# A fifth weight tile, gathers on GpSimd, one state buffer, and solve visits that wait for TensorE's instruction count

## The chip, the cores and the metric

The kernel runs on one core of a Trainium2 chip. The metric is the device time of one execution in microseconds; the median of several runs counts. Beside it stands one profiled execution, from which all views of the profile come.

## The reference

One step of a small decoder: an RWKV-7 layer (layer A) and an attention layer (layer B), on a prompt of 16 meta tokens and 256 tokens and on 8 single-token samples (280 columns in all), all in float32. Width of the model 2048, inner width 4096, 64 heads of 64.

```python
rkvz = jnp.einsum('btpd,pde->btpe', xm[:, :, :4], w_rkvz)      # four 2048 x 4096 products
w_log = -jax.nn.softplus(-(w0 + jnp.tanh(xw @ w1) @ w2)) - 0.5
decay = jnp.exp(-jnp.exp(w_log));  a = jax.nn.sigmoid(a0 + (xa @ a1) @ a2)
kk = normalized(k_h * k_k);  k_h = k_h * (1 + (a_h - 1) * k_a);  b_h = kk * a_h
def rwkv7_step(S, inp):                                         # scanned over the tokens, per head
    r, d, k, v, kk, b = inp
    sa = jnp.einsum('bhij,bhj->bhi', S, kk)
    S = S * d[:, :, None, :] - sa[..., None] * b[:, :, None, :] + v[..., None] * k[:, :, None, :]
    return S, jnp.einsum('bhij,bhj->bhi', S, r)
y = (group_norm(y) + bonus) * jax.nn.silu(z);  out_A = y @ w_out
k, v = shared_kv(h)                                             # for layer B
out_B = (banded attention with sinks(q, k, v) * jax.nn.silu(z)) @ w_o
```

Outputs are the normed hidden states, the recurrent states of prompt and samples, the shifts and the key and value caches.

## The kernel before

Activations lie transposed, features on partitions and the 280 columns along the free axis. Every large product is made of three TensorE passes (`mm3`): a weight tile `raw` of 128x512 comes in by DMA (`wunits`, line 200), ScalarE rounds it to `whi` (line 184), VectorE forms the rest `wlo` (line 186), and whi x xhi, whi x xlo, wlo x xhi are added in PSUM (lines 207 to 209). `raw` has 4 buffers, `whi` and `wlo` 5. SyncE's queue issues nearly all DMAs, in order.

Phase A (`phase_a`, `drive`) weaves layer A together. `products` runs 64 products (r, k, v, z in a fixed order, then the first half of the output product, `ps_o`), each in 16 pieces of six matmuls. `drive` turns a loop: at each turn every stream that is due issues its next part, and then one piece of a product follows. A stream says `yield n` (come back n turns later), or `yield n, condition`. TensorE's order is exactly the order of issue. The streams are:

- `main`: for each of eight groups of 8 heads (`o`) the scores of the odd unit, `substitute` (VectorE and POOL invert 16x16 triangles from the masked tile `ND`), `solve`, then `chain` (five steps over the tokens). `solve` makes the inverse larger in four visits to TensorE of short matmuls on 32-row quarters: two of 64 matmuls with 16 columns (lines 1082 and 1088), two of 32 matmuls with 32 columns (1100 and 1109), between them copies on VectorE and ScalarE. It begins `yield 24 if o < 5 else 27`, and `yield 4`, `7`, `5` stand between its visits.
- `preps`: prepares a unit of two pairs of heads: low-rank products `ps_l`, loads of `kT`, `rT`, `kk`, `vT`, and the gather of the samples' columns into `sm` by six ScalarE copies of 128x16 (line 910), which a transpose `ps_sm` (913) reads 8 turns later.
- `even_scores`, `group_norm` (transposes `ps_yt`, 1239, then the store of `yd`), `epilogues`.
- `decodes`: four groups of samples; each loads eight parts `dS` of the old state (1271), makes two products with each (1275), sums them (1276), and ends in a transpose `ps_dy` (1299).
- `late_gates`: once the last chain step and the fourth decode are done, splits the gated outputs of heads 32 to 63 into `ghi` and `glo` (lines 184, 186), which the second half of the output product, `ps_oa` in `out_a`, reads from its first matmul on.

In `scores`, ScalarE copies three 32-row parts of a score bank per half: two into `ND` (lines 997 and 998) and one into `N12` (999), a tile of its own; `solve` reads `N12` at line 1100.

Layer B (`phase_b`, `out_b`) follows with products `ps_kv`, `ps_q`, `ps_z`, `ps_ob`.

```python
# decode, before
S = rp.tile([128, NI, 64], F32, tag="dS", bufs=2, name=f"dS{g}_{q}")
...
dma(S.rearrange("p i j -> p (i j)"), I['state_wkv'][...])
yield 8 if g < 3 else 5, lambda: self.samples
for w, o in ((kk, sa), (dr, y)):
    tt(T, S, rowb(w), op=MU)
    V.reduce_sum(o[:, iq], T, axis=AX.X)
```

Of the kernel before, what the change touches and what calls it, by code (L numbers as in the profile page):

```python
# [107 lines left out]

class Kernel:
    def __init__(self, nc, tc, I, O):  # L110
        self.nc, self.tc, self.I, self.O = nc, tc, I, O
# [76 lines left out]
    def wunits(self, w, name, nk, col, nc_, per):  # L188
# [3 lines left out]
        for k0 in range(0, nk, per):  # L192
# [5 lines left out]
            else:  # L198
                raw = t("raw", F32, bufs=4)
# [5 lines left out]
    def mm3(self, ps, wh, wl, xh, xl, start, stop):  # L205
        mm = self.nc.tensor.matmul
# [23 lines left out]
    def gemm32(self, w, name, nk, cols, x):  # L230
# [4 lines left out]
        for k0 in range(0, nk, 2):  # L235
            for c, col in enumerate(cols):
# [3 lines left out]
                for k in range(2):  # L240
                    for i in range(2):
                        self.lead = self.nc.tensor.matmul(ps[2 * c + i][:, :N], raw[:, k, 128 * i:128 * i + 128],
                                                          x(k0 + k), start=k0 + k == 0, stop=k0 + k == nk - 1).ins
# [50 lines left out]
    def phase0(self):  # L294
# [23 lines left out]
        def filling(n):  # L318
            for _ in range(n):
                nc.tensor.matmul(junk[:, :N], ones, fill, start=True, stop=True)  # L320

        def summed(*ks):
            for k in ks:
                nc.tensor.matmul(pss[:, :N], ones, sq[:, k], start=k == 0, stop=k == KT - 1)
# [73 lines left out]
        def lora1():  # L398

            self.lt = []  # L400
            for m, wn, pool in ((4, 'a_w1', self.pc), (5, 'a_a1', self.pp)):
                ps = self.bank(pool, f"ps_{wn}")[:LR, :N]
                wv = self.I['lw'][:, m - 4]
                for k0 in range(0, KT, 4):
                    raw = lw0 if m == 4 and k0 == 0 else lw(f"{m}_{k0}")
                    dma(raw, wv[:, k0:k0 + 4])
                    for k in range(4):
                        if k % 2 == 0:
                            t = raw_part(m, (k0 + k) // 2)
                        nc.tensor.matmul(ps, raw[:, k], t[:, k % 2], start=k0 + k == 0, stop=k0 + k == KT - 1)  # L410
# [94 lines left out]
    def squares(self, p0, sqs):  # L505
        nc = self.nc
        pk = self.bank(self.py, f"ps_kk{p0}")
        for j in range(2):
            nc.tensor.matmul(pk[:, :N], self.sel[j], sqs[j], start=j == 0, stop=j == 1)
# [6 lines left out]
    def turn_v(self, p0, j, t, vk):  # L516
        nc = self.nc
        pt = self.bank(self.pe, name=f"ps_vt{p0}_{j}")
        for i, r in enumerate((128, 128, 16)):
            nc.tensor.transpose(pt[:r, i * 128:i * 128 + 128], t[:, j, i * 128:i * 128 + r], self.ident)  # L520
# [38 lines left out]
    def phase_a(self):  # L559
# [7 lines left out]
        self.ND = t([128, 20, 32], "ND")  # L567
# [6 lines left out]
        for a in (self.KB, self.ND, self.N16, self.Noff, self.Y):  # L574
            ms(a, 0.0)
# [229 lines left out]
    def end_k(self, p0, t):  # L805
# [6 lines left out]
        for j in range(2):  # L812
            nc.tensor.matmul(pk[:, :N], self.sel[j], sq[:, j], start=j == 0, stop=j == 1)
# [8 lines left out]
    def end_v(self, p0, t):  # L822
# [3 lines left out]
        for j in range(2):  # L826
            yield 3, self.pp_free
            pt = self.pp_bank(f"ps_vt{p0}_{j}")
            for i, r in enumerate((128, 128, 16)):
                nc.tensor.transpose(pt[:r, i * 128:i * 128 + 128], t[:, j, i * 128:i * 128 + r], self.ident)  # L830
# [5 lines left out]
    def prep(self, u):  # L836
# [72 lines left out]
        for i, x in enumerate((kk, a, kT, rT, vT, Pp[:, :, 5:])):  # L909
            A.copy(sm[:, :, i], x[:, :, L:N])  # L910
        yield 8, self.pp_free
        ps = self.pp_bank(f"ps_sm{u}")
        nc.tensor.transpose(ps[:96, :128], sm.rearrange("p a b c -> p (a b c)"), self.ident)
# [12 lines left out]
        for j in range(2):  # L926
            yield 5 - j if u > 1 else 3, self.pp_free
            ps = self.pp_bank(f"ps_bo{j}_{u}")
            nc.tensor.matmul(ps[:, :L], self.cr[C_BO], rk[j], start=True, stop=True)
# [30 lines left out]
    def scores(self, u):  # L960
# [15 lines left out]
        if u % 2 == 0:  # L976
            self.N12 = rp.tile([128, 16, 32], F32, tag="N12", name=f"N12_{u}")
        N12 = self.N12
# [3 lines left out]
        for c0 in (0, 2):  # L982
# [4 lines left out]
            with self.pe_order():  # L987
                for j in range(2):
                    for c in range(2):
                        for q in (1, 0):  # L990
                            o = 128 * (c0 + c)
                            nc.tensor.matmul(ps[q][:, j, c], KB[H(q), j, c0 + c, 64 * q:64 * q + 128],
                                             E[q][H(q), j, o:o + 128], start=True, stop=True)
            for q in range(2):
                pv, kr, br = ps[q], H(1 - q), H(q)
                r1, r2 = slice(64 * q, 64 * q + 32), slice(64 * q + 32, 64 * q + 64)
                A.copy(inst(self.ND, r1, cs), pv[r1, :, :, 0:32])
                A.copy(inst(self.ND, r2, cs), pv[r2, :, :, 32:64])
                A.copy(inst(N12, r1, cs), pv[r1, :, :, 32:64])
# [6 lines left out]
        with self.pe_order():  # L1006
            for j in range(2):
                for q in (1, 0):
                    nc.tensor.matmul(ps[q][:, j], KB[H(q), j, 4, 64 * q:64 * q + 128], E[q][H(q), j, 512:544],
# [13 lines left out]
        for j in range(2):  # L1023
            yield next(gap)
            ps = [b[:, :320].rearrange("p (c t) -> p c t", c=5) for b in banks(("bk", f"{j}_{u}"))]
            with self.pe_order():
                for c in range(5):
                    for q in (1, 0):
                        nc.tensor.transpose(ps[q][:, c], KB[H(q), j, c, 64 * q:64 * q + 128], self.ident[H(q), H(q)])
# [39 lines left out]
    def solve(self, o):  # L1069
# [16 lines left out]
        for i in range(16):  # L1086
            for q in range(4):
                nc.tensor.matmul(ps[32 * q:32 * q + 16, 256 + 16 * i:272 + 16 * i], ET[Q[q], i], TR[Q[q], :, i],
# [9 lines left out]
        for i in range(16):  # L1098
            for q in range(2):
                nc.tensor.matmul(ps[Q[2 * q + 1], i], self.N12[Q[2 * q], i], TN2[Q[2 * q], i], start=True, stop=True)  # L1100
# [5 lines left out]
        for i in range(16):  # L1106
            for q in range(2):
                r = Q[2 * q + 1]
                nc.tensor.matmul(ps[Q[2 * q], i], ET[r, i], TT[r, i, 32:64], start=True, stop=True)
# [27 lines left out]
    def chain(self, o):  # L1137
# [10 lines left out]
        mm = nc.tensor.matmul  # L1148
# [769 lines left out]
```

## Time and profile before

| | |
|---|---|
| median of 3 runs | 2190.12 us (2186.92 to 2193.9) |
| the profiled execution | 2201.98 us |
| its span | 2200.2 us |
| TensorE busy | 2122.6 us, 96% |
| VectorE busy | 1716.4 us, 78% |
| ScalarE busy | 1272.9 us, 58% |
| POOL busy | 83.4 us, 4% |
| mean granted clock of TensorE | 0.985 |

The views give times in microseconds from the span's start. A row of the time line reads: start, duration, engine, line of the code, operation, tiles written and read, shapes, count, and in brackets the idle time before it with what ended it. A row of the waits reads: total, times, longest. A row of a tile reads: minimum, median and maximum in ns, first and last start. A row of the stretches gives each engine's busy time with its number of instructions, the granted clock, and the share and rate of the DMA engines. "issue" is waiting for nothing that the profile shows. A DMA queue's row (q8) gives packets, MB and share.

### The profile page before, as it was taken

The page shows a single profiled execution, that of the slowest core. Times are in us where ns is not written, and L with a number is a line of the kernel's source. Part 1 is how long each engine was busy: PE and PEld are TensorE (multiplying, and loading weights), DVE is VectorE, ACT ScalarE, POOL GpSimd, SP SyncE. Part 2 cuts the span into 40 slices and gives each one's busy share as a digit, 9 for nine tenths or more (in the row PEclk, how much of TensorE's full clock was granted, in tenths as well). Part 3 has the DMA queues.
Part 4 walks back from the last instruction along what each step waited for, and adds up shares of the span by engine and source line. Part 5 has one row for each costly group of instructions (what it writes and reads, how often), then busy time and mean ns, then how long its engine had stood idle before and what let it go on. Part 6 is the DMA issues. An engine that isn't in the chain of part 4 may idle for free.

```text
span 2200.2 us, 56108 instructions
## 1 busy us (share of the span) xinstructions
PE 2122.6 (96%) x21556; PEld 2015.7 (92%) x21556; DVE 1716.4 (78%) x4115; ACT 1272.9 (58%) x2916; POOL 83.4 (4%) x100
## 2 busy tenths in 40 slices
PE   9999999999999998999999999999999999999997
PEld 7998899999889898888889899998999999999997
DVE  7956767787587776877887786997888888888885
ACT  3456756675666656756666454564565556555443
POOL 0010000000000000100001000110000000000000
PEclk9999999999999999999999999999999999999999
DMA  6997667757656776665645878766554544577774
GB/s 235 320 316 233 191 192 236 210 175 258 198 171 187 235 226 178 203 196 173 207 138 156 276 228 251 241 213 200 157 160 139 168 145 135 167 209 242 231 225 136
DMA packets 277444, 448.51 MB, mean 204 GB/s; under 512 B 53352, under 2 KB 99112, under 8 KB 276784
## 3 DMA queue, kind: packets, MB, share of 16 engines
q1 hardware_dynamic: 276888, 443.89, 65.1%
q8 instruction: 169, 2.77, 0.5%
q10 hardware_dynamic: 288, 1.05, 0.1%
q14 instruction: 99, 0.81, 0.1%
HBM read 382.81 MB, written 66.15 MB: 204 GB/s over the span
## 4 chain that ended last, share of the span: by engine, by line
PE 82%; DMA 6%; DVE 6%; ACT 4%; issue 2%; SPq 0%; DVEq 0%; POOLq 0%; ACTq 0%
PE ps_z L207 6%; PE ps_z L208 5%; PE ps_z L209 5%; PE ps_ob L209 3%; PE ps_ob L208 3%; PE ps_v L207 3%; PE ps_ob L207 3%; PE ps_q L209 3%; PE ps_q L207 3%; PE ps_q L208 3%; PE ps_k L207 3%; PE ps_v L208 3%; PE ps_v L209 3%; PE ps_k L209 2%; PE ps_k L208 2%; PE ps_r L207 2%
## 5 line engine op out<-in xcount | busy, mean ns | idle before, releaser
L207 PE MATMUL ps_z<-mhlm,whi_z 128*128 128x280 f32 x512 | 160.9, 314 | 1.1 <-ACT st L770 1.1
L208 PE MATMUL ps_z<-mhlm,whi_z 128*128 128x280 f32 x512 | 152.2, 297 | 2.1 <-issue 2.1
L207 PE MATMUL ps_q<-bmh,whi_qb 128*128 128x264 f32 x512 | 150.5, 294 | 2.4 <-ACT whi_qb L184 2.4
L209 PE MATMUL ps_z<-mhlm,wlo_z 128*128 128x280 f32 x512 | 152.0, 297 | 0.0
L209 PE MATMUL ps_q<-bmh,wlo_qb 128*128 128x264 f32 x512 | 146.7, 286 | 1.5 <-DVE wlo_qb L186 1.5
L207 PE MATMUL ps_z<-bmh,whi_zb 128*128 128x264 f32 x512 | 147.5, 288 | 0.0
L208 PE MATMUL ps_q<-bml,whi_qb 128*128 128x264 f32 x512 | 146.1, 285 | 0.0
L208 PE MATMUL ps_z<-bml,whi_zb 128*128 128x264 f32 x512 | 145.5, 284 | 0.0
L209 PE MATMUL ps_z<-bmh,wlo_zb 128*128 128x264 f32 x512 | 145.5, 284 | 0.0
L207 PE MATMUL ps_ob<-ghi,whi_ob 128*128 128x264 f32 x512 | 145.3, 285 | 0.0
L209 PE MATMUL ps_ob<-ghi,wlo_ob 128*128 128x264 f32 x512 | 144.9, 285 | 0.0
L208 PE MATMUL ps_ob<-glo,whi_ob 128*128 128x264 f32 x512 | 144.5, 283 | 0.0
L186 DVE TENSOR_TENSOR wlo_r<-raw_r,whi_r 128x512 fp32r<-128x512 f32 x128 | 87.8, 688 | 64.9 <-ACT whi_r L184 63.9
L184 ACT CAST whi_oa<-raw_oa 128x512 fp32r<-128x512 f32 x128 | 78.9, 620 | 101.2 <-DMA raw_oa<-a_w_out 31.7
L184 ACT CAST whi_ob<-raw_ob 128x512 fp32r<-128x512 f32 x128 | 79.2, 621 | 97.1 <-PE ps_ob L208 80.2
L186 DVE TENSOR_TENSOR wlo_v<-raw_v,whi_v 128x512 fp32r<-128x512 f32 x128 | 87.9, 691 | 53.0 <-ACT whi_v L184 48.7
L207 PE MATMUL ps_k<-mhlm,whi_k 128*128 128x280 f32 x384 | 121.9, 317 | 1.9 <-ACT whi_k L184 1.6
L207 PE MATMUL ps_v<-mhlm,whi_v 128*128 128x280 f32 x384 | 121.4, 316 | 1.9 <-ACT st L770 1.9
L186 DVE TENSOR_TENSOR wlo_z<-raw_z,whi_z 128x512 fp32r<-128x512 f32 x128 | 88.6, 695 | 35.7 <-ACT whi_z L184 32.7
L186 DVE TENSOR_TENSOR wlo_oa<-raw_oa,whi_oa 128x512 fp32r<-128x512 f32 x128 | 87.5, 689 | 35.4 <-ACT whi_oa L184 31.7
L186 DVE TENSOR_TENSOR wlo_k<-raw_k,whi_k 128x512 fp32r<-128x512 f32 x112 | 76.0, 687 | 49.5 <-ACT whi_k L184 49.1
L184 ACT CAST whi_zb<-raw_zb 128x512 fp32r<-128x512 f32 x128 | 78.3, 619 | 62.5 <-PE ps_z L208 42.0
(462 smaller groups left out, 7739.5 us busy)
## 6 DMA issues: line engine op xcount, KB each, us to landing
raw_k<-a_w_rkvz SPq DMA_DIRECT2D x128, 256.0 KB
raw_v<-a_w_rkvz SPq DMA_DIRECT2D x128, 256.0 KB
raw_r<-a_w_rkvz SPq DMA_DIRECT2D x128, 256.0 KB
raw_z<-a_w_rkvz SPq DMA_DIRECT2D x128, 256.0 KB
raw_oa<-a_w_out SPq DMA_DIRECT2D x128, 256.0 KB
raw_qb<-b_w_qz SPq DMA_DIRECT2D x128, 256.0 KB
raw_zb<-b_w_qz SPq DMA_DIRECT2D x128, 256.0 KB
raw_ob<-b_w_o SPq DMA_DIRECT2D x128, 256.0 KB
```

What stands on the lines that cost most here:

```text
L184: self.nc.scalar.copy(hi, src)
L186: return self.nc.vector.tensor_tensor(lo, src, hi.bitcast(F32), op=ALU.subtract)
L207: mm(ps, wh, xh, start=start, stop=False)
L208: mm(ps, wh, xl, start=False, stop=False)
L209: return mm(ps, wl, xh, start=False, stop=stop)
```

## The change

Five things change. `raw` has 5 buffers. The six gathers into `sm` go from ScalarE to GpSimd. `ND` and `N12` become the two halves of one tile `F`, so that one copy of 64 columns takes the place of two of 32. `dS` has one buffer; its load comes 3 turns after the products of the part before, and these follow 5 turns later (4 in the fourth group). And a wrapper `TensorE` counts every matmul and transpose that is issued, with an assumed duration, in blocks of 256 instructions; the first two visits of `solve` ask it ahead of each quarter whether the rest of the visit leaves the block at least 5000 ns long, and otherwise come back a turn later.

```diff
+class TensorE:
+    BLOCK = 256
+    def __init__(self, tensor):
+        self.tensor, self.n, self.at = tensor, 0, 0.0
+        self.left = 190.0
+    def count(self, n, ns):
+        self.n += n
+        self.left -= n * 1.004
+        self.at += ns
+        if self.left <= 0:
+            self.left += self.BLOCK
+            self.at = 0.0
+    def matmul(self, out, lhsT, rhs, **k):
+        c = 1
+        for x in rhs.shape[1:]:
+            c *= x
+        exact = rhs.dtype == F32
+        self.count(4 if exact else 2, (17 if c <= 16 else 33 if c <= 32 else 68 if c <= 64 else c) if exact else c * .46)
+        return self.tensor.matmul(out, lhsT, rhs, **k)
+    def transpose(self, out, in_, ident):
+        self.count(2, 45)
+        return self.tensor.transpose(out, in_, ident)
+    def room(self, n):
+        m = min(n, self.left)
+        return self.at + 4.3 * m + 64 * (self.left - m) >= 5000
...
-                raw = t("raw", F32, bufs=4)
+                raw = t("raw", F32, bufs=5)
...
-        self.ND = t([128, 20, 32], "ND")
+        self.F = t([128, 20, 64], "F")
+        self.ND, self.N12 = self.F[:, :, 0:32], self.F[:, 0:16, 32:64]
...
-            A.copy(sm[:, :, i], x[:, :, L:N])
+            G.tensor_copy(sm[:, :, i], x[:, :, L:N])
...
-                A.copy(inst(self.ND, r1, cs), pv[r1, :, :, 0:32])
+                A.copy(inst(self.F, r1, cs), pv[r1, :, :, 0:64])
                 A.copy(inst(self.ND, r2, cs), pv[r2, :, :, 32:64])
-                A.copy(inst(N12, r1, cs), pv[r1, :, :, 32:64])
...
         for i in range(16):
+            while i % 4 == 0 and not self.te.room(256 - 16 * i):
+                yield 1
             for q in Q:
-                nc.tensor.matmul(ps[q, 16 * i:16 * i + 16], Noff[q, i], TN[q, :, i], start=True, stop=True)
+                self.te.matmul(ps[q, 16 * i:16 * i + 16], Noff[q, i], TN[q, :, i], start=True, stop=True)
...                                       # the same loop around the second visit
         for q in range(64 // NI):
-            S = rp.tile([128, NI, 64], F32, tag="dS", bufs=2, name=f"dS{g}_{q}")
+            if q:
+                yield 3
+            S = rp.tile([128, NI, 64], F32, tag="dS", bufs=1, name=f"dS{g}_{q}")
...
-            yield 8 if g < 3 else 5, lambda: self.samples
+            yield 5 if g < 3 else 4, lambda: self.samples
```

Every other `nc.tensor.matmul` and `nc.tensor.transpose` becomes `self.te.matmul` and `self.te.transpose`, with the same operands.

More of the change, by code (lines that the diff above doesn't have):

```diff
@@ L409, in lora1 @@
                             t = raw_part(m, (k0 + k) // 2)
[L410 removed]
+                        self.te.matmul(ps, raw[:, k], t[:, k % 2], start=k0 + k == 0, stop=k0 + k == KT - 1)
                     if k0 < KT - 4:
@@ L1414, in out_a @@
             if k >= KT - 2:
-                nc.tensor.matmul(pst[:, :N], ones, acc if k == KT - 2 else sq, start=k == KT - 2,
+                self.te.matmul(pst[:, :N], ones, acc if k == KT - 2 else sq, start=k == KT - 2,
                                  stop=k == KT - 1)
```

74 lines of the change are left out of this document (37 added, 37 removed).

## The prediction

> **What bounds the kernel now.** I read the page's head first, then TensorE's waits, then the clock by stretch, then the places the change touches.
>
> ```profile
> span 2200.2 us, 56108 instructions
> PE 2122.6 (96%) x21556; PEld 2015.7 (92%) x21556; DVE 1716.4 (78%) x4115; ACT 1272.9 (58%) x2916; POOL 83.4 (4%) x100
> q8 instruction: 169, 2.77, 0.5%
> PE 82%; DMA 6%; DVE 6%; ACT 4%; issue 2%; SPq 0%; DVEq 0%; POOLq 0%; ACTq 0%
> ```
>
> TensorE is busy 96% of the span and carries 82% of the chain: time is won only where it idles or runs slowly. Each recorded matmul has a weight load beside it, so 2 x 21556 instructions came in 169 fetches, 255 each: a block is 256.
>
> ```profile
> PE ps_so L1088 <- issue: 5.5, 4, 1.8
> PE ps_z L208 <- issue: 2.1, 1, 2.1
> PE ps_o L207 <- issue: 2.0, 1, 2.0
> PE ps_so L1109 <- ACT ET L1104: 4.6, 3, 1.9
> PE ps_vt L830 <- ACT ta L861: 2.9, 2, 2.0
> PE ps_so L1088 <- DVE ET L1084: 2.3, 1, 2.3
> PE ps_v L207 <- ACT st L770: 1.9, 1, 1.9
> PE ps_sy L1184 <- ACT X L1183: 1.6, 1, 1.6
> ```
>
> In TensorE's waits (total, times, longest) 9.6 us are "issue": nothing in the profile was awaited. The rest are short waits for ScalarE and VectorE. Nearly all lie in phase A, whose clock the stretches show (PEclk stands behind the engines, before DMA share and GB/s):
>
> ```profile
> 350.00:650.00 300.00, 291.16 (x3490) 271.06 (x3489) 225.48 (x521) 198.58 (x490) 12.89 (x16) 0.97 0.66 208
> 650.00:950.00 300.00, 284.51 (x3560) 265.39 (x3558) 230.03 (x521) 192.60 (x454) 14.18 (x12) 0.98 0.69 207
> 950.00:1240.00 290.00, 270.70 (x3492) 252.81 (x3493) 230.06 (x512) 181.78 (x425) 13.32 (x12) 0.97 0.60 187
> 411.50:414.80 3.30, 3.30 (x16) 3.21 (x15) 3.30 (x6) 2.11 (x5) 0.00 (x0) 0.50 0.76 200
> 804.10:807.40 3.30, 3.30 (x16) 3.30 (x16) 1.83 (x3) 1.11 (x3) 0.00 (x0) 0.50 0.50 143
> 831.40:834.70 3.30, 3.30 (x14) 3.30 (x15) 3.05 (x9) 0.41 (x2) 0.00 (x0) 0.50 1.04 343
> 967.90:974.60 6.70, 6.70 (x92) 6.37 (x88) 2.77 (x5) 3.02 (x7) 0.00 (x0) 0.50 0.61 165
> 1097.60:1100.90 3.30, 3.30 (x16) 3.27 (x15) 1.83 (x3) 1.35 (x4) 0.00 (x0) 0.50 0.63 204
> ```
>
> TensorE idles 8.8, 15.5 and 19.3 us there, and the clock loss adds 9, 6 and 8.7 us. The last five rows show how: stretches of about 3.3 us (one of 6.7) at half clock, half of which is lost, about 1.7 us for a short one. The one at 804.1 begins right behind this stall:
>
> ```profile
> 800.79 0.93 PE L1088 MATMUL ps_so<-TR,ET 32*16 32x16 f32 x91
> 802.87 0.48 PE L1088 MATMUL ps_so<-TR,ET 32*16 32x16 f32 x37 [1.16 <-issue]
> ```
>
> The 128 records (256 instructions, one block) of a solve's visit need only 0.93 + 0.48 us. The stall sits in their middle, and the only thing that comes in such blocks is the code itself.
>
> **The hold (`room`).** It removes the cause of 9.6 us if the count hits the true borders. I take 8, for some drift of the count; bounds 0 and 9.6. The half-clock stretches at 804 and 1098, both behind a second visit's stall, go with it: 2 x 1.7 = 3.4.
>
> Its price is lateness. `main` is paced by its own yields: chain 48 turns of the drive, odd scores 21, solve 40 (43 from the fifth), all else behind them. A turn emits one piece, six product matmuls; 64 products of 16 pieces make 1024. I counted both kernels' turns and instructions by the code's yields and conditions, positions only. For the kernel before, the fourth decode's ps_dy comes at piece 962, the last ps_yt at 988, the last gate at 992: 32 turns of room. For the changed kernel each visit is checked four times. Example, first solve: 42 instructions left, at 13682 ns, so it starts; after 64 instructions it is in a new block, 192 to go, 234 left, and 4.3 x 192 + 64 x 42 = 3514 is under 5000. A piece adds 773 ns and takes 12 instructions, so little changes until 192 are left, then 721 are gained each: five turns. The eight solves give 5+1, 6+2, 2+1, 5+2, 3+2, 0+8, 0+8, 0+8: **53 turns**, all kept to the end, since `main` waits for nobody. The last ps_yt moves to 1041, 17 turns past the last product. The fourth decode starts 53 later too, and its eight loads now need 7 turns each instead of 5: ps_dy at 1030, gates at 1036 to 1046. All gates, which the first ps_oa needs, fall behind the last product. What happens there now (the time line; the row of four casts is the tile ghi's):
>
> ```profile
> 1300.55 0.27 PE L1299 MATMUL ps_dy<-consts,dy 128*64 128x128 f32 x1
> 1305.13 1.13 ACT L184 CAST ghi<-gy 128x1120 fp32r<-128x1120 f32 x1 [0.68 <-DVE gy L1367]
> 1323.49 0.49 PE L1239 MATMUL ps_yt<-consts,Y 128*128 128x128 f32 x3
> L184 ACT CAST ghi<-gy x4: 1122/1124/1129, 1305.1 to 1337.1; 128x1120 fp32r<-128x1120 f32 x4
> 1353.48 0.29 PE L207 MATMUL ps_oa<-ghi,whi_oa 128*128 128x280 f32 x1
> ```
>
> A turn lasts (1353.48 - 1300.55) / 62 = 0.85 us here. The last state step (emitted 16 turns before ps_dy) would come 10 turns, 8.5 us, before the products end, and its arithmetic takes 16 turns (13.7 us) as now: ps_dy stands 5 us past the end. From ps_dy to the end of the first ghi are 1306.26 - 1300.55 = 5.7 us. So TensorE has nothing to do for 11 us. From the last ps_yt to the last ghi are 1338.2 - 1323.5 = 15 us, against about 9 us until its first use in ps_oa; some 2 us of stall follow. Idle TensorE brings at least one half-clock stretch, 1.7. Together 15, and 2 for the loads below: **17 us**, bounds 0 (if everything is early) and 26.
>
> **One state buffer.** A load may now start only when the second product of the step before has read the tile (the time line, then two pieces of the chain of waits, start and length):
>
> ```profile
> 1258.55 0.68 DVE L1275 TENSOR_TENSOR dT<-dS,ve 128x512 f32<-128x512 f32 x1
> 1259.99 0.69 DVE L1275 TENSOR_TENSOR dT<-dS,ddr 128x512 f32<-128x512 f32 x1
> 741.58 5.94 DMA raw_k<-a_w_rkvz
> 747.58 9.82 DMA raw_k<-a_w_rkvz
> ```
>
> Two products last 2.1 us, the load of 256 KB 5 to 10 us (raw tiles of the same size on the chain, thus late ones; I take 5). The sum, 7 to 8 us, is above the seven turns of the fourth decode (6 to 7) and under the eight of the others (9 at their 1.18 us, 1210 us by 1024 turns). Behind the waiting load stand raw loads on SP's queue; behind the waiting product stand the lo splits on VectorE. Besides the 2 us in the tail I take 1; bounds 0 and 8.
>
> **Gathers to POOL.** On ScalarE they cost little by themselves and much by what they wait for (the rows of the tile sm with the idle time ahead of its readers and writers, then the time line):
>
> ```profile
> L910 ACT COPY sm<-vT x16: 198/204/208, 158.3 to 1099.7; 128x16 f32<-128x16 f32 x16
>   DMA rT<-rd: 24.7, 15
>   DMA vT<-vd: 15.2, 8
> 945.46 0.20 ACT L910 COPY sm<-vT 128x16 f32<-128x16 f32 x1 [3.12 <-DMA vT<-vd]
> 949.31 0.69 DVE L186 TENSOR_TENSOR wlo_z<-raw_z,whi_z 128x512 fp32r<-128x512 f32 x1 [4.74 <-ACT whi_z L184]
> 951.21 1.24 PE L1088 MATMUL ps_so<-TR,ET 32*16 32x16 f32 x128 [2.27 <-DVE ET L1084]
> ```
>
> 96 copies of 0.2 us are 19 us, and ScalarE stood 40 us in front of them for two loads. The last three rows are the damage: ScalarE waits 3.12 us for vT, VectorE then 4.74 for ScalarE, and TensorE 2.27. The five listed waits for ScalarE and VectorE are 13.3 us; looking back up to 7 us on ScalarE's time line, such a gather stands ahead of all but one of the three for ET L1104 (1.35, half of what its longest leaves) and the longer one for ta (2.0): 10 us. I take 8, bounds 0 and 13. Half-clock stretches follow such waits at 411, 831 and 968 (two long): 4 x 1.7 = 6.8, of which I take 5. On POOL the copies get in front of the masks on which the solve rests; the nearest row bounds one from above, ScalarE's 0.2 us from below:
>
> ```profile
> L1411 POOL COPY sqacc<-sqa 128x280 f32<-128x280 f32 x1 | 0.4, 427 | 73.5 <-ACT sqa L1408 73.5
> ```
>
> Six are 1.2 to 2.6 us per unit, inside the 8 turns left for them ahead of ps_sm; POOL is 4% busy. Cost 1, bounds -1 and 5.
>
> **Copies.** Two of 256 ns become one twice as wide; at equal width 16x256 took 363:
>
> ```profile
> L998 ACT COPY ND<-ps_sc x64: 256/257/263, 192.1 to 1190.6; 32x128 f32<-32x128 f32 x64
> L1092 ACT COPY TT<-ps_so x16: 362/364/366, 270.4 to 1230.9; 16x256 f32<-16x256 f32 x16
> ```
>
> 64 x 150 ns are 9.6 us off ScalarE, off the path; with 19 us of gathers gone as well, I credit 4 us of the remaining short waits (0 to 10). **The fifth raw tile** starts each load one unit earlier; I credit 3 us (0 to 6) for late raw loads like the 9.82 above.
>
> **The sum.** Gains 8 + 3.4 + 8 + 5 + 4 + 3 = 31; costs 17 + 1 + 1 = 19. The profiled execution took 2201.98 us (span 2200.2) and would take 2190. The median of the runs, 2190.12, lies 11.9 below it; the same 12 us off give **2178**. 0.3% is 6.6 us, about what a measurement can tell.
>
> **Rivals.** *Slower, the tail decides:* the single state buffer makes each of the last seven loads 2 us later (9.8 us for a landing), so ps_dy, and with it every gate, comes 14 us later than I put it, and the waits merely move: costs 33, and of the gains the 5, 4 and 3 that I only credited don't come, 19 left: 2204. It decides once the tail exceeds the gains, 31 us at my values. For it: 53 turns against 32 of room, and nothing in the code brings `main` forward. Against: the decode's VectorE work gets thinner when no products run. *The hold does nothing:* the stalls are not fetches, or the count misses them: without 11.4 us of gain it is 2190, no change. The stall inside one instruction's run speaks against it. The Trainium skill, in "Runtime: NRT & Kernel Launch", section "Instruction fetch mechanics", says that the next 16 KiB block of 256 instructions is fetched while the present one runs and that crossing is mostly hidden; by it the hold is worth nothing. The trace agrees on the size and not on the hiding (1.16 us in mid-visit). *The tail is hidden:* the gates still come early, 17 us less: 2161. *The gathers stall POOL:* the masks wait behind vT, and the solve with them: the 13 us of that item are lost, 2191. The skill's "SBUF — State Buffer", section "Who interferes with whom", has a VectorE operation with two SBUF inputs block against a POOL read; no run here shows it for such copies.
>
> **How the numbers follow.** Forecast 0.45, slower rival 0.27, idle hold 0.12, hidden tail 0.08, POOL 0.08. The forecast's own spread is 11 us either way, so a fifth of it is no change and a twentieth slower. Faster: 0.34 + 0.08 + 0.05 from the edges of the others = 0.47. Slower: 0.27 + 0.02 + 0.04 = 0.33. Same: 0.20. The range reaches from the hidden tail to just past the slower rival, 2161 to 2206; the faster cases' own range is 2161 to 2183.
>
> **What would show it.** The issue rows of ps_so gone; no gather on ScalarE, and its waits for rT and vT on POOL; the half-clock stretches fewer; eight solves drifting late, the last ps_dy and ps_yt behind the last ps_o, and a gap of 11 to 20 us ahead of the first ps_oa. If that gap is missing, my turns are wrong; if phase A's products end no earlier than now, the gains are.

## The result, and the profile after

| | before | after |
|---|---|---|
| median | 2191.13 us (6 runs, 2186.92 to 2194.7) | 2164.4 us (6 runs, 2158.35 to 2172.02) |
| ratio | 1 | 0.988 (95% interval 0.9856 to 0.9905) |
| profiled execution | 2201.98 us | 2161.31 us |

The change makes the kernel 26.7 us faster. The prediction said faster, by 12 us. The two profiled executions lie 40.7 us apart, because that of before was 11 us above its median and that of after 3 below; so terms of a few us are taken from the medians of runs below, not from these two traces.

The head of the page after, and the engines of its chain:

```profile
span 2159.5 us, 56146 instructions
PE 2104.0 (97%) x21556; PEld 2003.4 (93%) x21556; DVE 1714.4 (79%) x4115; ACT 1258.4 (58%) x2756; POOL 137.0 (6%) x196
PE 75%; DMA 5%; DVE 4%; ACT 2%; issue 1%; SPq 0%; DVEq 0%; POOLq 0%; ACTq 0%; POOL 0%
```

160 instructions left ScalarE (96 gathers, 64 copies), and 96 came to POOL. The three stretches of phase A that the prediction showed, in the kernel after:

```profile
350.00:650.00 300.00, 297.57 (x3617) 278.99 (x3616) 233.34 (x543) 199.79 (x455) 32.25 (x44) 1.00 0.69 214
650.00:950.00 300.00, 290.33 (x3755) 272.61 (x3754) 241.07 (x537) 199.37 (x432) 26.26 (x38) 0.99 0.70 219
950.00:1240.00 290.00, 282.36 (x3647) 265.27 (x3647) 237.80 (x517) 179.67 (x390) 19.58 (x30) 0.99 0.64 196
```

TensorE now idles 2.4, 9.7 and 7.6 us (8.8, 15.5 and 19.3 before), and the clock is at 1.00, 0.99 and 0.99 (0.97, 0.98, 0.97). TensorE's waits (total, times, longest), some rows:

```profile
PE ps_oa L130 <- ACT ghi L217: 4.8, 1, 4.8
...
PE ps_so L130 <- DVE TN L1091: 2.6, 2, 2.3
...
PE ps_wu L130 <- ACT X L1234: 2.4, 4, 0.8
...
PE ps_sm L134 <- POOL sm L944: 2.3, 1, 2.3
...
PE ps_z L130 <- issue: 1.4, 1, 1.4
```

The "issue" waits on ps_so are gone (before: 5.5 us), of the others one of 1.4 us is left. A new wait leads the list: the first reader of the late gate's cast `ghi`. (In this kernel every matmul is issued from the wrapper's line 130 and every transpose from line 134, so go by the tiles.) The tile ps_oa, first and last start, before and then after:

```profile
L209 PE MATMUL ps_oa<-ghi,wlo_oa x256: 287/292/299, 1353.7 to 1452.7; 128*128 128x280 f32 x128
```

```profile
L130 PE MATMUL ps_oa<-ghi,wlo_oa x256: 286/292/435, 1303.1 to 1417.6; 128*128 128x280 f32 x128
```

Up to the first ps_oa the profiled execution gains 50.6 us (1353.7 to 1303.1); the ps_oa stage, taken here and below from the first to the last start of this row, loses 15.5 (99.0 becomes 114.5: the tail); layer B gains the remaining 5.6. That sets the questions: what gave 50.6, and was it the hold, which also made the tail?

### The profile page after: what moved, and what is told of

Same layout as the page of the kernel before. It is cut to its first block, busy times and chain, and to the rows that moved or that the text cites. A ratio compares the mean times of both kernels' runs of the same rounds, so it can differ in the third digit from the quotient of the medians.

```text
span 2159.5 us, 56146 instructions
## 1 busy us (share of the span) xinstructions
PE 2104.0 (97%) x21556; PEld 2003.4 (93%) x21556; DVE 1714.4 (79%) x4115; ACT 1258.4 (58%) x2756; POOL 137.0 (6%) x196
## 4 chain that ended last, share of the span: by engine, by line
PE 75%; DMA 5%; DVE 4%; ACT 2%; issue 1%; SPq 0%; DVEq 0%; POOLq 0%; ACTq 0%; POOL 0%
PE ps_z L130 18%; PE ps_ob L130 9%; PE ps_q L130 7%; PE ps_k L130 7%; PE ps_r L130 5%; PE ps_v L130 5%; PE ps_oa L130 4%; PE ps_o L130 3%; PE ps_sy L130 3%; PE ps_wu L130 2%; PE ps_kv L130 2%; PE ps_so L130 2%; PE ps_at L130 1%; PE ps_sc L130 1%; DMA dS<-state_wkv 1%
## 5 line engine op out<-in xcount | busy, mean ns | idle before, releaser
L130 PE MATMUL ps_z<-mhlm,whi_z 128*128 128x280 f32 x1024 | 210.8, 301 | 2.7 <-issue 1.4
L130 PEld LDWEIGHTS ps_z<-mhlm,whi_z 128*128 128x128 f32 x1024 | 162.4, 189 | 8.2 <-issue 1.8
L130 PE MATMUL ps_v<-mhlm,whi_v 128*128 128x280 f32 x768 | 160.4, 303 | 0.0
L130 PE MATMUL ps_k<-mhlm,whi_k 128*128 128x280 f32 x768 | 158.4, 301 | 0.0
L130 PEld LDWEIGHTS ps_v<-mhlm,whi_v 128*128 128x128 f32 x768 | 121.4, 189 | 4.3 <-ACT st L804 0.2
L130 PEld LDWEIGHTS ps_k<-mhlm,whi_k 128*128 128x128 f32 x768 | 121.5, 188 | 4.1
L217 ACT CAST whi_v<-raw_v 128x512 fp32r<-128x512 f32 x128 | 78.7, 618 | 65.3 <-PE ps_v L130 30.4
```

The lines of the kernel that those rows point to most:

```text
L130: return self.tensor.matmul(out, lhsT, rhs, **k)
L217: self.nc.scalar.copy(hi, src)
```

## The experiments

Two theories at the start. A: ScalarE's relief (gathers, copies) is the gain that was sized too small. B: the hold is the large gain. C, that the fifth raw tile is, stood as an outsider. Times below are medians beside the kernel before on the same chip; differences in us between runs of different sets go by their ratios to it (0.001 is 2.2 us).

### The hold

Without it, all else kept:

```diff
-            while i % 4 == 0 and not self.te.room(256 - 16 * i):
-                yield 1
```

> The changed kernel without the two waits of the solve's long visits; fifth raw tile, gathers on POOL, merged copies and the single state buffer stay. The first ps_oa stage falls back from 115 to about 99.5 us (16 us won), since main is no longer late. Theory A (ScalarE's relief is the gain that I sized too small, some 35 us of it): only the six issue stalls and two half-clock stretches return, 10 to 13 us, so the time is about 2160 (2157 to 2165), and the products still end about 1310 us. Theory B (the hold is the large gain: it takes away fetch stalls and, with them, most half-clock stretches, 35 us and more): the products end at 1340 us and the time is about 2185. Prediction as on record: 11.4 us of gain gone and 17 of cost gone, 2159.

Measured: 2155.92 us, ratio 0.9849 (0.9826 to 0.9873), that is faster than the full change. TensorE's waits and the ps_oa stage of this run:

```profile
PE ps_so L130 <- issue: 3.0, 4, 1.3
...
PE ps_r L130 <- issue: 1.8, 1, 1.8
```

```profile
L130 PE MATMUL ps_oa<-ghi,wlo_oa x256: 287/292/299, 1314.6 to 1413.5; 128*128 128x280 f32 x128
```

The products end 11.5 us later than with the hold (1314.6 beside 1303.1), and the stage is 15.6 shorter (98.9 beside 114.5). Theory B falls: in this pair of traces the hold brings 11.5 us, where 11.4 was on record, and its tail costs more. The hold alone, on the kernel before:

> The kernel before with the instruction count and the waits of the long visits alone; four raw tiles, gathers on ScalarE, separate copies, two state buffers. Theory A: the issue stalls and two half-clock stretches go (11 us), the late gates cost 16, so about 2196 (2192 to 2200). Theory B: 35 us go and 16 come, about 2172. Both expect a first ps_oa stage of some 115 us and no issue wait on ps_so L1088.

Measured: 2192.39 us, ratio 1.0025 (1.001 to 1.0039), so 5.5 us slower than before. By the ratios the hold loses about 6 us in both surroundings (with the other parts present the two intervals overlap; alone it is clear). Two more pairs with and without it follow at the end, and they differ: the products end 7.8 and 18 us earlier with it, the stage is 10 and 14 us longer, and the times lie 2.4 us behind and 1.3 us ahead, within the noise. So the gain is 8 to 18 us and the price 10 to 16, by single traces, and what is left depends on the rest of the kernel.

Is it the block's border that counts, or only that the visit is spread over more turns? The count moved by half a block:

```diff
-        self.left = 190.0
+        self.left = 62.0
```

> The changed kernel with the count's start moved by half a block (62 instead of 190 instructions left), all else the same; main is then late by some 30 turns instead of 40. If the stalls in the solve's visits are fetches at true block borders: visits run into the border again, issue waits on ps_so come back (3 or more, 5 us), the products end at about 1310 instead of 1302.6, and the first ps_oa stage is 5 us or so shorter: 2162 to 2168. If only the spreading of the visits' instructions over more turns matters and not where the borders lie: no issue waits, products still end at 1303, the shorter tail shows: 2154 to 2160.

Measured: 2168.61 us, ratio 0.9917 (0.9903 to 0.9931).

```profile
PE ps_so L130 <- issue: 2.7, 4, 1.7
...
PE ps_k L130 <- issue: 1.3, 1, 1.3
```

```profile
L130 PE MATMUL ps_oa<-ghi,wlo_oa x256: 286/292/435, 1315.2 to 1424.6; 128*128 128x280 f32 x128
```

Four waits on ps_so are back, and the products end at 1315.2, as with no hold at all. So the stalls sit at true borders of 256 instructions (the returned waits show it; the end of the products alone wouldn't, as the next run shows), and a count that is half a block off keeps most of the price (a stage of 109.4 us) without the gain. The Trainium skill, in "Runtime: NRT & Kernel Launch", section "Instruction fetch mechanics", calls crossing such a border mostly hidden. The runs agree on the 256 and not on the hiding: the four waits on ps_so before are 1.4 us in the mean and 1.8 at most, in visits whose 256 instructions take 1.4 us.

The tail: its last steps drawn together.

```diff
-            yield 3 if j else 36 if o < NU // 2 - 1 else 19
+            yield 3 if j else 36 if o < NU // 2 - 1 else 8
-            yield (6 if b == G1 else 3), self.after(4, ('g', b))
+            yield (2 if b == G1 else 1), self.after(2, ('g', b))
```

> The changed kernel with its last steps drawn together: 8 instead of 19 turns ahead of the last ps_yt, the gates 2, 1, 1 turns apart instead of 6, 3, 3, two turns behind the state they wait for instead of four. If the tail (115 instead of 99.5 us for the first ps_oa stage) is a matter of the last turns, as in the prediction: the stage takes 100 to 106 us and the time is 2150 to 2156. If the last gate waits for transfers and VectorE anyway: 2160 to 2165.

Measured: 2165.28 us, ratio 0.9906 (0.9891 to 0.9921): nothing won, as the second expectation said. The first ps_oa comes at 1313.9 in place of 1302.7, the stage is 110 us long: about 5 us left the stage and 11 came ahead of it, though no issue wait on ps_so came back. The runs don't show what moved it.

### Gathers and copies

The gathers alone, on the kernel before:

```diff
-            A.copy(sm[:, :, i], x[:, :, L:N])
+            G.tensor_copy(sm[:, :, i], x[:, :, L:N])
```

> The kernel before with one line changed: the gathers of the tile sm go to POOL. Theory A: the short waits of TensorE behind ScalarE and half-clock stretches after them go, 20 to 30 us: 2161 to 2171. Theory B: these waits are rare and others take their place: 2185 to 2191. On record the gathers were worth 8 + 5 - 1 = 12 us: 2179. The issue stalls on ps_so stay in all three.

Measured: 2180.55 us, ratio 0.9975 (0.9958 to 0.9992): 5.5 us, less than half of what was on record, and far from theory A. The waits went on. ScalarE's waits for phase A's raw tiles in this run (the same rows of before stand further down):

```profile
ACT whi_v L184 <- DMA raw_v<-a_w_rkvz: 35.5, 24, 3.9
...
ACT whi_k L184 <- DMA raw_k<-a_w_rkvz: 24.0, 11, 7.1
ACT whi_r L184 <- DMA raw_r<-a_w_rkvz: 23.8, 16, 3.8
...
ACT whi_z L184 <- DMA raw_z<-a_w_rkvz: 10.5, 8, 2.8
```

94 us, where the kernel before has 65. The likely reading is that ScalarE, freed from the gathers, comes sooner to a raw tile that has not landed, and stands there; both traces are of executions some 10 us above their medians. The copies alone (`ND` and `N12` as one tile `F`, one copy where two were):

> The kernel before with the two tiles ND and N12 as one and 64 pairs of copies merged. On record: about 10 us of ScalarE's time off the path, with the gathers' 19 us worth 4; so 2183 to 2187. If the run without the hold (10 us under the run with the raw tile alone) and the run with the gathers alone (5 us) add up, the copies are worth 5: 2182. If the copies cost (a single tile ties the solve's stages together, since the next pair's copies wait for the last reader of the tile): 2190 or more.

Measured: 2183.08 us, ratio 0.9979 (0.9968 to 0.999): 4.6 us. Theory A falls as well.

### The fifth raw tile

With it came the single state buffer, which pays for its room, and the decode's yields:

```diff
-                raw = t("raw", F32, bufs=4)
+                raw = t("raw", F32, bufs=5)
...
+            if q:
+                yield 3
-            S = rp.tile([128, NI, 64], F32, tag="dS", bufs=2, name=f"dS{g}_{q}")
+            S = rp.tile([128, NI, 64], F32, tag="dS", bufs=1, name=f"dS{g}_{q}")
...
-            yield 8 if g < 3 else 5, lambda: self.samples
+            yield 5 if g < 3 else 4, lambda: self.samples
```

> The kernel before with the fifth raw tile, the single state buffer that pays for it, and the decode's changed yields. Theories A and B: 2191 within 4 us (3 us of earlier loads against 1 to 3 us of later decode). Theory C (late raw loads are behind many of the splits' delays, and the fifth tile takes them away): 2175 to 2181.

Measured: 2164.63 us, ratio 0.9897 (0.9876 to 0.9919): 22.5 us, more than all else together, and below the ranges of all three theories. Three parts were changed at once here, so they were taken apart. Tile and single buffer with the old yields:

> The kernel before with the fifth raw tile, paid for with a single state buffer, and the decode's yields left as they were (8 or 5 turns behind each load, none ahead of it). Theory C, now the main one: ScalarE's casts stand in front of raw loads (109 us in 73 waits in the kernel before, 56 us in 40 with the tile and the yields changed), all ScalarE's other work stands behind these casts, and the fifth tile takes half of that away: 2166 (2161 to 2171), ScalarE's waits for raw tiles at 50 to 60 us. Theory D (the decode's changed yields are the gain: its VectorE work falls on other stages of the solve): 2185 to 2191.

Measured: 2193.11 us, ratio 1.0029 (1.0015 to 1.0043): slower than before, which neither theory C in its simple form nor D had said. What theory C said of the waits did come true: ScalarE's for raw tiles are 57.5 us over the whole kernel, and the four rows of phase A sum to 18, where before has 65:

```profile
ACT whi_k L184 <- DMA raw_k<-a_w_rkvz: 10.7, 6, 2.9
...
ACT whi_v L184 <- DMA raw_v<-a_w_rkvz: 4.8, 4, 1.6
...
ACT whi_z L184 <- DMA raw_z<-a_w_rkvz: 1.4, 2, 1.0
ACT whi_r L184 <- DMA raw_r<-a_w_rkvz: 1.3, 1, 1.3
```

So fewer of these waits do not by themselves make a faster kernel; the single buffer stood against them here. Single buffer and yields without the tile:

> The complement: four raw tiles, the single state buffer and the decode's changed yields. Theory C: 2185 to 2192, ScalarE's waits for raw tiles stay above 95 us. Theory D: 2166 (2161 to 2171).

Measured: 2184.16 us, ratio 0.9985 (0.9973 to 0.9997). Neither half has the 22.5 us. If effects simply add, one number follows that no run had yet given: the single buffer alone must cost 24.

> The kernel before with one state buffer in place of two, nothing else. The three runs of the raw tile's parts gave +6 us (fifth tile and single buffer), -3 (single buffer and the decode's changed yields) and -21 (all three). Theory E: the effects add. Then the single buffer with the old yields costs 6 - 3 + 21 = 24 us (VectorE waits for landings, and the lo splits stand behind it), the fifth tile is worth 18 and the yields 27, mostly by repairing that: 2211 (2203 to 2218). Theory F: the single buffer costs little, and the fifth tile pays only together with the yields: 2185 to 2194.

Measured: 2210.76 us, ratio 1.0109 (1.0093 to 1.0125): the 24 us of theory E. And the yields alone, with two buffers:

> The kernel before with the decode's changed yields (three turns ahead of each load, five behind it), two state buffers and four raw tiles. Theory E in its plain form, the yields only repair what the single buffer breaks: 2184 to 2190. Theory G (the yields put the decode's VectorE work at better places by themselves, the first ps_dy comes at 474 us instead of 584): 2160 to 2175, since the run with the single buffer and these yields was 3 us faster in spite of the buffer.

Measured: 2177.49 us, ratio 0.9958 (0.9943 to 0.9973): 9 us, between the two expectations. So the yields do more than repair; how they bring 9 us by themselves the runs don't show. The parts now close: **the tile is worth 17.5 us** (1.0029 against 1.0109) **to 19** (0.9897 against 0.9985), **the yields 9, and the single buffer costs 6** beside the new yields (0.9985 against 0.9958) and 24 beside the old. VectorE's wait for a state, single buffer alone and then with the new yields:

```profile
DVE dT L1275 <- DMA dS<-state_wkv: 36.1, 14, 3.9
```

```profile
DVE dT L1277 <- DMA dS<-state_wkv: 15.6, 12, 4.0
```

Why the tile? One tile fewer shows the other side:

> The kernel before with three raw tiles in place of four, nothing else. Theory C: slower by at least as much as the fifth tile is faster, 2215 or more, with ScalarE's waits for raw tiles at 180 us or more and more half-clock stretches. Theory D: three suffice nearly as four do, 2188 to 2200.

Measured: 2237.36 us, ratio 1.0222 (1.0209 to 1.0235): 49 us slower, as theory C said. ScalarE's waits for phase A's raw tiles, with three, four (before) and five of them (the run of tile, buffer and yields):

```profile
ACT whi_v L184 <- DMA raw_v<-a_w_rkvz: 60.9, 48, 3.9
...
ACT whi_k L184 <- DMA raw_k<-a_w_rkvz: 45.6, 31, 7.5
...
ACT whi_r L184 <- DMA raw_r<-a_w_rkvz: 44.3, 33, 4.4
...
ACT whi_z L184 <- DMA raw_z<-a_w_rkvz: 33.3, 29, 3.2
```

```profile
ACT whi_k L184 <- DMA raw_k<-a_w_rkvz: 22.0, 12, 7.1
...
ACT whi_r L184 <- DMA raw_r<-a_w_rkvz: 20.8, 12, 3.6
...
ACT whi_v L184 <- DMA raw_v<-a_w_rkvz: 13.8, 15, 3.0
...
ACT whi_z L184 <- DMA raw_z<-a_w_rkvz: 8.2, 7, 1.9
```

```profile
ACT whi_v L184 <- DMA raw_v<-a_w_rkvz: 12.8, 6, 3.0
...
ACT whi_z L184 <- DMA raw_z<-a_w_rkvz: 3.2, 4, 1.8
ACT whi_r L184 <- DMA raw_r<-a_w_rkvz: 3.2, 2, 2.4
...
ACT whi_k L184 <- DMA raw_k<-a_w_rkvz: 3.0, 3, 1.5
```

184, 65 and 22 us in sum. So more tiles make ScalarE wait less for them, and three pairs of runs show that they shorten the time. How the one brings the other shows only in part in the waits. None of TensorE's wait rows in these runs names such a tile, but a cast that stands on ScalarE for a late tile holds back all that ScalarE does behind it, among it what the chain and the solve need. TensorE's waits for ScalarE fit this in two pairs: 53.1 us with three tiles and 34.6 with four, 26.9 and 16.8 without and with the fifth beside the new yields. Beside the old yields they stay (34.8 and 34.9), and those for VectorE fall instead (29.2 to 21.8).

Nor is a wait of ScalarE worth its own length: 119 us more of them cost 49 us (three tiles for four), and 52 us fewer brought 19. Between runs that differ in other things their sum doesn't order the times at all: with the yields alone it is 79 us where before has 65, and the kernel is 9 us faster than before.

The chain of work that ended last, which a page shows in shares, says it more plainly. Between 140 and 1300 us the loads of r, k, v and z tiles on it sum to 103 us with three tiles, 55 before, and 55, 60 and 43 with four tiles in the runs of the single buffer, of buffer and yields, and of the yields; with five they are 8 us with the old yields and 8 with the new. So the tile takes these loads off the chain. (The trace of the hold alone, with four tiles, has a chain without any load.) The loads of states stand on it only with one buffer: 63 us with the old yields, 12 with the new, none before. A chain's time is not won whole when a piece leaves it, because the next chain is nearly as long.

A rival is that with a fifth buffer SyncE's queue stands less, and the other loads come sooner. It gets no support: beside the new yields ScalarE's waits for rT and vT rise with the tile from 31.4 to 39.2 us, VectorE's for states from 15.6 to 16.5.

The tile also works in layer B. The tile ps_q, first and last start, in the run with single buffer and yields and in that with the fifth tile as well:

```profile
L209 PE MATMUL ps_q<-bmh,wlo_qb x512: 279/284/586, 1490.6 to 1816.9; 128*128 128x264 f32 x171
```

```profile
L209 PE MATMUL ps_q<-bmh,wlo_qb x512: 279/284/390, 1478.9 to 1800.8; 128*128 128x264 f32 x171
```

326.3 and 321.9 us: 4.4 us of the tile's 18 come from there. One matmul of 586 ns, twice the median, is gone with them.

### What is left of the tail, and the best version

A shorter chain gives `main` its turns back, with and without the hold:

```diff
-            yield (5 if c else 3), (None if c or not o else self.after(2, ('g', o - 1)))
+            yield (4 if c else 3), (None if c or not o else self.after(2, ('g', o - 1)))
```

> The changed kernel with four of the five waits of each chain step block one turn shorter (4 instead of 5), which gives main 4 turns back per solve, 32 in all, of the 40 that the hold makes it late. Theory L (the hold's whole price is main's lateness, paid in the first ps_oa stage): the products still end near 1303, the stage is 99 to 104 us, the time 2148 to 2154. Theory M (the chain's steps then come too close and TensorE waits for W and X instead): 2160 or more, with longer waits on ps_wu and ps_sy.

> The control for it: the same shorter chain without the hold. Theory L: main was not late, so nothing is won: 2153 to 2160 as without the shorter chain, issue waits on ps_so present, first ps_oa stage 99.5. Theory M: slower, 2160 to 2168.

Measured: 2173.86 us, ratio 0.9942 (0.9924 to 0.9959), and 2170.82, ratio 0.9931 (0.9914 to 0.9947). Theory M: the row of the first is

```profile
PE ps_wu L130 <- ACT X L1234: 12.1, 7, 4.0
```

beside 2.4 us before this edit, and its stage is still 109 us. The state loads made smaller, so that three buffers fit and a load comes two steps ahead, without the hold (the last line sums up the ones added):

```diff
-        NI = 8
+        NI = 4
...
-            S = rp.tile([128, NI, 64], F32, tag="dS", bufs=1, name=f"dS{g}_{q}")
+            # load(q + 2) ahead of step q, from "dS" with bufs=3; yield 4 (3 in the last group) per step
```

> The changed kernel without the hold, and with the decode's states in 64 steps of 128 KB in place of 32 of 256 KB: three small buffers with loads two steps ahead take less room than one large one with its product tile. Effects added: the single buffer costs 24 us with the old yields and 7 with the changed ones (the run with the yields alone was 9.5 us faster than before, with the single buffer 3). If that is the wait for landings, VectorE's waits for dS go and the time is 2147 to 2152 in place of 2156. If the number of VectorE's operations or SP's issues matters more: 2158 or more.

> The changed kernel with the hold, the shorter chain and the small state buffers. Effects added: 2164 - 13 (lateness given back) - 6 (no wait for states) = 2145 (2140 to 2150). If either of the two fails on its own, the other's sum.

> The changed kernel (hold included, chain waits of 5 turns as they are) with the small state buffers and loads two steps ahead. The runs so far don't add: the small buffers were worth nothing without the hold (2157 beside 2156) but 22 us beside hold and shorter chain (2152 beside 2174); the shorter chain cost 10 us with and 15 without the hold. If the small buffers pay wherever main is late (VectorE's waits for dS then fall on the solve): 2146 to 2154. If they pay only with the shorter chain: 2160 to 2166.

Measured: without the hold 2156.93 us, ratio 0.986 (0.9845 to 0.9875), nothing won, though VectorE's waits for states fell from 18 to 3.4 us; with the hold and the old chain 2155.47, ratio 0.9854 (0.9834 to 0.9875), 6 us better than the changed kernel's ratio (the intervals overlap); with the hold and the shorter chain 2152.2, ratio 0.9837 (0.982 to 0.9854). These are not additive: the shorter chain costs 14 to 18 us with the large states and nothing measurable with the small ones; the sum of 2145 on record for both was missed by 7. The place of the decode's work against the solve may decide here; the runs don't settle it.

Last, the late gates' loads from POOL's queue, on the version with the hold, the old chain and the small states. SyncE's queue in the changed kernel, from the last gate's store on (start, length, line, transfer):

```profile
1308.08 0.55 SPq L1277 DMA_DIRECT2D yd<-vT  x1
...
1312.08 4.23 SPq L233 DMA_DIRECT2D raw_oa<-a_w_out  x6
1316.98 0.57 SPq L1393 DMA_DIRECT2D gy<-yd  x1
```

The load of the last gate's y goes out 9 us after the store that it needs.

> The same with the loads of the last two gates (y and z from DRAM) issued from POOL's queue in place of SP's. In the changed kernel the load of y for the last gate left SP at 1316.98, 9 us after the last store that it needs, behind eight issues of raw_oa; and TensorE stood 4.8 us for its cast. Theory N (SP's order is the tail): the first ps_oa stage gets 4 to 10 us shorter than in the run beside it, which it beats by as much. Theory O (the gate waits for VectorE and for the other gate's buffer): within 2 us of it.

Measured: 2152.87 us, ratio 0.9845 (0.9825 to 0.9866), not to be told from the run beside it (2155.47); the stage took 112.2 us in place of 113.3. POOL's queue in that run:

```profile
1309.07 0.77 POOL L1399 DMA_DIRECT2D gy<-yd  x1 [14.94 <-DMA raw_oa<-a_w_out]
```

The store had left SyncE at 1301.76, so even with a queue of its own the load went out 7.3 us later, although POOL had nothing else to do: it waited, it seems, for the store to land (the releaser that the row names, a raw tile, is not among what this load needs; that the store is meant is inferred, and the 4.2 to 7.7 us from issue to landing of these stores and loads fit it). So the queue is not the tail, as theory O said; that the way of y through DRAM is what remains of it is inferred from these rows and not tested.

The best of these versions are at 0.984 to 0.985, 2152 to 2156 us, their intervals over one another. The run that only leaves out the hold (2155.92) is the simplest of them.

## Why the prediction was right or wrong

By its own steps, in us; gains positive:

| step | on record | measured | from |
|---|---|---|---|
| hold: stalls and the clock behind them | 8 + 3.4 | 11.5 | products' end with and without it |
| hold: the tail | -17 | -15.6 | ps_oa stage with and without it |
| gathers: waits, clock, POOL | 8 + 5 - 1 | 5.5 | alone, on the kernel before |
| ScalarE's relief by copies | 4 | 4.6 | copies alone |
| fifth raw tile | 3 | 17.5 to 19 | two pairs of runs |
| single state buffer | -1 | -6 | beside the new yields |
| decode's yields | no term | 9 | yields alone |

The right column adds to 11.5 - 15.6 + 5.5 + 4.6 + 18 - 6 + 9 = 27, and the change measured 26.7. That it comes so near is luck: the two rows of the hold come from one pair of traces, and with the 6.8 us that the medians give for it the sum is 24. No run had the fifth tile beside two state buffers, so its row holds beside the single one.

**The step that failed is the fifth raw tile**: "I credit 3 us (0 to 6) for late raw loads like the 9.82 above". It showed two raw loads of the chain that ended last and priced such loads at 3 us; between 140 and 1300 us that chain holds eight loads of r, k and v, 55 us in sum, of which the fifth tile leaves 8. The rows that mattered were in the waits of ScalarE, an engine at 58%: 109 us in 73 waits over the whole kernel, 65 of them in the four rows shown above. The same page had led me to charge the gathers' 40 us of such waits with 13 us, by looking back from TensorE's stalls; the raw tiles' waits, more than twice as many, were not looked at in this way. Measured, taking away the gathers' waits was worth 5.5, while 29 us of waits for raw tiles came up (65 to 94), probably in their place; with the fifth tile 52 us of those went (74 us in the four rows with single buffer and yields, 22 with the tile as well), worth 13 to 15 in phase A. The look back from a stall had named the nearest wait ahead of it, not the supply behind that.

**The yields had no term at all.** They were read as the single buffer's companion. Alone they bring 9 us, and without them the buffer costs 24. The bound that the prediction set for the buffer (0 to 8) held with the yields (6) and would have failed without.

**The hold was right in both halves, by the pair of traces with and without it.** The cause (borders, by the shifted run), the gain and the price came out as on record, and so did that its price exceeds its gain; the other pairs above allow 8 to 18 and 10 to 16. The turns were not right: counted by the product matmuls ahead of it in the trace, six to a turn, the last ps_dy comes at turn 1017 and not 1030, the last ps_yt at the end and not 17 turns past it. The last three solves' second visits were held by about two turns, not eight. The last solve comes 41 turns later than before, with all parts and with the hold alone, not 53; and without the hold it still comes 13 turns later than before, so `main` does wait for others, which the prediction denied. Nor is there the gap of 11 to 20 us ahead of the first ps_oa that would have shown it: the early gates let the stage begin, and the price lies inside it. The time line there, and two of its stretches:

```profile
1321.89 0.29 PE L130 MATMUL ps_oa<-ghi,wlo_oa 128*128 128x280 f32 x1
1327.01 0.84 PE L130 MATMUL ps_oa<-ghi,whi_oa 128*128 128x280 f32 x2 [4.83 <-ACT ghi L217]
```

```profile
1315.60:1318.90 3.30, 3.30 (x15) 3.30 (x15) 0.00 (x0) 0.00 (x0) 0.00 (x0) 0.50 1.03 272
1325.80:1332.60 6.80, 5.07 (x20) 4.74 (x21) 1.98 (x3) 1.90 (x4) 0.00 (x0) 0.50 0.00 0
```

One wait of 4.83 us for the last cast, and two stretches at half clock with 8.4 us of work, half of which is lost. Over the whole stage TensorE idles 9.5 us at a clock of 0.96 (0 and 1.00 before). The size was near for a reason that was partly another, and so partly by luck: less lateness, but 22.6 us from the last ps_yt to the end of the last `ghi`, where the prediction took the 15 us of before and "some 2 us of stall"; 9 us of them lie between the store's issue and the load's on SyncE's queue.

**Rivals.** The slower one (the tail decides) failed on both sides: the last ps_dy came 13 turns earlier than forecast and not 14 us later, the tail cost 15.6 us and not 31, and the gains were larger. The tail is hidden: its 2161 lies near the 2164.4 measured, but by luck, since the stage did grow by 15.5 us. The hold does nothing: as a cause refuted by the shifted run, though in time the gain is eaten. The gathers stall POOL: with the gathers alone moved, TensorE's waits for POOL are 1.6 us and VectorE's 2.9, as before; with the whole change one TensorE wait of 2.3 us for POOL's `sm` stands. The solve was not held up by them.

## What to carry to other kernels

Sum the waits of each engine that serves the bottleneck by what they wait for, however little busy the engine is: 109 us in front of transfers showed where a deeper buffer was worth 18 us, twice what the other edits came to together. The sum says where to search, not what it is worth; only runs gave the price. When a buffer is paid for by another's, price both, and price the yields that come with them: here the tile was worth 18 us beside the single buffer, the buffer cost 24 with the old yields and 6 with the new, and the yields alone brought 9. And a wait that keeps an instruction stream off a fetch border is only worth its gain if the stream that waits has room to be late.

## What the runs showed of the hardware

A POOL copy of 128x16 that takes 0.2 us can take 4.0. The rows of the tile sm (minimum, median, maximum in ns) and one copy with VectorE's time line beside it, kernel after:

```profile
L944 POOL COPY sm<-vT x16: 197/199/1236, 156.4 to 1077.2; 128x16 f32<-128x16 f32 x16
L944 POOL COPY sm<-kk x16: 197/914/4031, 158.2 to 1100.3; 128x16 f32<-128x16 f32 x16
```

```profile
192.12 4.03 POOL L944 COPY sm<-kk 128x16 f32<-128x16 f32 x1 [7.47 <-DVE kk L910]
196.10 0.19 POOL L944 COPY sm<-Pp 128x16 f32<-128x16 f32 x1
```

```profile
191.98 1.32 DVE L922 TENSOR_TENSOR_SCAN cl<-reset,cl 128x272 f32<-128x272 f32 x2
193.23 0.66 DVE L219 TENSOR_TENSOR wlo_r<-raw_r,whi_r 128x512 fp32r<-128x512 f32 x1
...
196.12 0.21 DVE L990 TENSOR_TENSOR E<-rT,Pp 128x32 f32<-128x32 f32 x1
196.26 0.67 DVE L1030 TENSOR_TENSOR E<-ps_sc,consts 64x512 f32<-64x512 f32 x1
```

From 191.98 on VectorE runs operations with two SBUF inputs without a pause, and the copy lasts until nearly the end of that row of operations, 0.1 us before the first one that reads PSUM (the next copy fits beside the last of them in 0.19 us). It is not one case: of the 96 copies 41 took over 0.5 us, and in each of them such VectorE operations ran for some 80% of the copy or more; of the 48 under 0.3 us they ran for over half of it in 8. The prediction said that no run there showed this; this one does, though no run tested it by itself. The Trainium skill states it in "SBUF — State Buffer", section "Who interferes with whom": a VectorE operation with two SBUF inputs contends with a POOL instruction that reads SBUF.

And the price of spacing: with one buffer in place of two, the same eight state loads per group cost 24 us or 6, by three turns that stand ahead of each load instead of behind it (in the fourth group there are also two more in all).
